# Low parts of the projection weights on VectorE in two halves, in a hybrid attention and recurrence step

## The chip, the cores and the metric

The kernel runs on one core of a Trainium2 chip. The core has five engines that run side by side, each through its own queue and in that queue's order: TensorE (PE in the profile, its weight loads PEld), VectorE (DVE), ScalarE (ACT), GpSimd (POOL) and SyncE (SP), which here issues the DMAs. The metric is the device time of one execution in microseconds (us), lower being better. The kernel before takes 2957.14 us, the median of three runs (2954.69 to 2958.95).

## The reference

One step of a diffusion backbone, one layer deep: 1024 latent tokens and 128 context tokens of width 1024 go through a feed-forward half step, a token mixer and a second feed-forward half step. All of it is float32. The mixer has two branches over the same input `h`, and each begins with a slice of one large projection:

```python
def token_mixer(h, cache, lb, w_in, ...):
    qc, kvc, kr, hq, hf_f, hf_b, hi, hgate, ga, gr = jnp.split(h @ w_in, split_idx, axis=-1)
    ...                                                  # attention: qc, kvc, kr
    q_h, v_h = jax.nn.silu(heads(hq)), heads(hi)
    f_fw = lb_h[0] + (1.0 - lb_h[0]) * jax.nn.sigmoid(heads(hf_f))
    f_bw = lb_h[1] + (1.0 - lb_h[1]) * jax.nn.sigmoid(heads(hf_b))
    o_fw, s_fw = hgrn2_chunked(q_h, 1.0 - f_fw, jnp.log(f_fw), v_h, s0[:, 0])
    o_bw, s_bw = hgrn2_chunked(flip(q_h), flip(1.0 - f_bw), flip(jnp.log(f_bw)), flip(v_h), s0[:, 1])
    o_rec = rmsnorm(o_fw + flip(o_bw), hg_norm_g) * jax.nn.silu(heads(hgate))
    merged = jax.nn.sigmoid(ga) * (o_attn @ w_up_attn) + jax.nn.sigmoid(gr) * (o_rec @ w_up_rec)
    return merged @ w_out
```

The recurrence has eight heads of 64 by 64. It carries a state S with S_t = diag(f_t) S_(t-1) + k_t v_t, where k_t = 1 - f_t, and reads it with q_t, once forwards and once backwards in time.

## The kernel before

Activations lie transposed: the 1024 features on 128 partitions in eight tiles, the 1152 tokens along the free axis, taken in three chunks of 384 (`ORDER` is 2, 0, 1).

**Split matrix products.** TensorE takes its operands as float32r, which holds fewer bits than float32. So each operand is split into a high part, which is its rounding, and a low part, which is the rest. A product becomes three (`mm3`, lines 447 to 449): high weight by high input, high weight by low input, low weight by high input. For a weight, `load_w` issues the DMA into a tile `raw` (line 241, two buffers), and `hl` makes the parts: ScalarE copies `raw` into `wh` (line 235), then GpSimd subtracts `wh` from `raw` into `wl` (line 236). `wh` and `wl` have three buffers each. A projection weight is one tile of 128 partitions by 8 by 128, so 1024 values on each partition.

**The stage of the recurrence** (`hgrn`) is where most of the changed loads are used. It computes 36 slices of the projection, each 72 matrix products: eight of the forget gates (`proj_f`), four each of queries, values and output gates (`proj_q`, `proj_v`, `proj_gate`), and sixteen of the gates that merge the branches (`proj_sg`). They are generators that yield after each half of a chunk, 12 matrix products. Between these pieces the scan of one head is woven in: `scan_pre` prepares a chunk, `scan_lev` combines blocks over four doublings, `scan_out` reads out a head. At most four slices are run per head while its three chunks are scanned.

**The scan's chain** goes over all engines. `scan_pre` forms `X` and `Y` (products of gates and their reciprocals, lines 804 to 811), the keys and queries `Kb` and `Qb` (lines 816 and 817, VectorE, two halves of the partitions each), the block factors `TK`, `TQ` and their product (lines 821 to 825), `KE` on VectorE (829) and `QP` on GpSimd (830). Each level of `scan_lev` has TensorE multiply blocks into the PSUM tile `lv` (862), then VectorE and GpSimd scale `KE` and `QP` in place (898: three parts on VectorE, one on GpSimd), VectorE multiplies the factors `T` (899), and ScalarE copies key halves `kr` (874, 875) and finished blocks `Af` (906, 907, 912). The next level's matrix products need these. The state is carried in `scan_out` (line 936). After every second head `rec_norm` normalises the output, with logarithm and exponential on ScalarE, which loads a table of functions for each.

**What sets the order.** The code is written as one program, and the framework plans each engine's queue from it, by priorities and by its own idea of how long things take; the queues in the trace therefore do not follow the program's text line by line. Loads run ahead of their use as far as free buffers allow. Instructions wrapped in `pin` keep their written order; none of the loads changed here is pinned. On the chip every queue runs in the order planned.

The first forget gate's weight is loaded with `home="pieces"`: ScalarE copies and VectorE subtracts in two halves (lines 227 and 228). All other projection loads take the last branch of `hl`.

Of the kernel before, what the change touches and what calls it, by code (L numbers as in the profile page):

```python
# [10 lines left out]
F32R = mybir.dt.float32r  # L11
# [8 lines left out]
P = 128  # L20
D = 1024
KT = D // P
# [66 lines left out]
class Trunk:  # L89
# [125 lines left out]
    def hl(self, raw, shape, eng=None, pin=lambda i: i, home=None):  # L215
        if home == "half":
            wh, wl = [[self.half(n, F32R)[:, : D // 2] for _ in range(2)] for n in ("wxh", "wxl")]
            for v in range(2):
                src = raw[:, 0, ts(v, D // 2)]
                self.nc.scalar.copy(wh[v], src)  # L220
                self.nc.gpsimd.tensor_sub(wl[v], src, wh[v])
            return wh, wl
        if home == "pieces":
            wh, wl = [self.wp.tile(shape, F32R, tag=t, bufs=3, name=t) for t in ("wh", "wl")]
            for v in range(2):
                k = slice(4 * v, 4 * v + 4)
                self.nc.scalar.copy(wh[:, k], raw[:, k])
                self.nc.vector.tensor_sub(wl[:, k], raw[:, k], wh[:, k])
            return wh, wl
        if home:  # L230
            wh, wl = [home(n)[:, :D].rearrange("p (o d) -> p o d", o=1) for n in ("wxh", "wxl")]
        else:
            wh = self.wp.tile(shape, F32R, tag="wh", bufs=3, name="wh")
            wl = self.wp.tile(shape, F32R, tag="wl", bufs=3, name="wl")
        pin(self.nc.scalar.copy(wh, raw))  # L235
        pin((eng or self.nc.gpsimd).tensor_sub(wl, raw, wh))  # L236
        return wh, wl
# [94 lines left out]
    def alloc_h(self):  # L332
        hl = [(self.tt(F32R, f"xh{k}"), self.tt(F32R, f"xl{k}")) for k in range(KT)]
        self.xh, self.xl = zip(*hl)
# [134 lines left out]
    def down(self, ws, hs, gm, c, m, tag="dn", bufs=3):  # L469
        nc = self.nc  # L470
        lo, hi = span(c)
        cs = slice(lo, hi)
        ps = self.pp.tile([P, hi - lo], F32, tag=tag, bufs=bufs, name=tag)
        self.mm3(ps, [(wh, wl, hh[:, cs], hl[:, cs]) for (wh, wl), (hh, hl) in zip(ws, hs)])
        for a, b, s in segs(c):
            nc.vector.scalar_tensor_tensor(  # L476
                self.x[m][:, a:b],
                ps[:, a - lo : b - lo],
                self.modt[:, gm, m, s : s + 1],
                self.x[m][:, a:b],  # L480
                ALU.mult,
                ALU.add,
            )
# [39 lines left out]
    def down_final(self, ws, hs, gm):  # L523
# [4 lines left out]
        for lo, hi in FINAL:  # L528
# [5 lines left out]
            def terms(m):  # L534
                w = [(rows(wh, m), rows(wl, m)) for wh, wl in ws]
                return [(wh, wl, hh[:, lo:hi], hl[:, lo:hi]) for (wh, wl), (hh, hl) in zip(w, hs)]
# [110 lines left out]
    def proj_f(self, i, h, out):  # L647
        nc = self.nc
        fs = out["f"] = self.tt(F32, "fs")
        nc.vector.memset(fs[64:P, 0:1], 1.0)  # L650
        w = self.load_w(self.a["w_in"][i], KT, P, home="pieces" if i == 0 else None)
        for c in ORDER:
            s = self.sigm((yield from self.proj_g(w, c)))
            lo, hi = c * CW, (c + 1) * CW
            for r, o in ((slice(0, 64), 0), (slice(64, P), 1)):
                nc.scalar.activation(
                    fs[r, lo + o : hi + o], s[r], AF.Identity, scale=self.lb1[r, h : h + 1], bias=self.lb[r, h : h + 1]
                )
            yield

    def proj_q(self, i, out):
        q = out["q"] = self.tt(F32, "q")
        w = self.load_w(self.a["w_in"][i], KT, P)
        for c in ORDER:
            ps = yield from self.proj_g(w, c)
            self.nc.vector.tensor_mul(q[:, c * CW : (c + 1) * CW], ps, self.sigm(ps))  # L666
            yield

    def proj_v(self, i, out):
        nc = self.nc  # L670
        V = out["V"] = self.tt(F32, "V")
        w = self.load_w(self.a["w_in"][i], KT, P)
        for c in ORDER:
            ps = yield from self.proj_g(w, c)
            t = self.fp.tile([P, CW], F32, tag="t", bufs=3, name="t")
            nc.scalar.copy(t, ps)
            pt = self.pp.tile([P, CW], F32, tag="sm", bufs=3, name="vt")
            for j in range(3):
                nc.tensor.transpose(pt[:, ts(j, P)], t[:, ts(j, P)], self.ident)
            nc.scalar.copy(V[:, c * CW : (c + 1) * CW], pt)  # L680
            yield

    def proj_gate(self, i, p, oT):
        nc = self.nc
        w = self.load_w(self.a["w_in"][i], KT, P)
        sq = self.tt(F32, "osq")[:, :T]
        nc.scalar.activation(sq, oT[:, :T], AF.Square)
        for c in ORDER:
            ps = yield from self.proj_g(w, c)
            if c == ORDER[0]:  # L690
                self.lnexp()
                for b in ORDER:
                    self.rec_norm(b, oT, sq)
            s = self.sigm(ps)
            nc.vector.tensor_mul(s, ps, s)
            cs = slice(c * CW, (c + 1) * CW)
            nc.gpsimd.tensor_mul(s, oT[:, cs], s)
            nc.sync.dma_start(self.orec[p][:, cs], s)
            yield

    def proj_sg(self, j):
        w = self.load_w(self.a["w_in"][20 + j], KT, P)
        for c in ORDER:
            s = self.sigm((yield from self.proj_g(w, c)))
            self.nc.sync.dma_start(self.sg[j // KT, j % KT][:, c * CW : (c + 1) * CW], s)
            yield
# [1127 lines left out]
```

## Time and profile before

| | |
|---|---|
| median of three runs | 2957.14 us (2954.69 to 2958.95) |
| the profiled execution | 2961.18 us, its span 2959.4 us |
| mean granted TensorE clock | 0.985 |
| TensorE busy | 2839.9 us of the span |
| VectorE, ScalarE, GpSimd busy | 1993.1, 1285.5, 1035.0 us |
| line 236 on GpSimd, `wl`, all stages | 106 operations, 238.6 us |
| the recurrence's stage | about 850 to 1460 us after the start |

A row of a group reads: line, engine, operation, the tile written, an arrow, the tiles read, shapes, count, then busy time in us and the mean of one in ns, then the idle time of the engine just before these operations and what ended it. A row of the waits reads: who waited, for whom, the sum in us, how often, the longest. A row of the timeline reads: start and length in us, engine, line, operation, tiles, count, and in brackets the idle time before it and its releaser. A row of stretches gives the busy time of each engine in that stretch, the granted clock, and the DMAs' share.

### The profile page before, as it was taken

How to read it: one execution, taken by the hardware profiler on the slowest of the kernel's cores; microseconds unless marked ns; L12 is line 12 of the kernel's file. 1: busy time of each engine (PE TensorE's matmuls, PEld its weight loads, DVE VectorE, ACT ScalarE, POOL GpSimd, SP SyncE). 2: the span in 40 equal slices, each digit the busy share in tenths (PEclk: the TensorE clock that was granted, in tenths of full speed). 3: DMA queues.
4: the chain of work that ended last, by engine and by line, in shares of the span. 5: the costliest groups of instructions: out<-in, count | busy, mean ns of one | idle time of the engine just before them, and what ended most of it. 6: DMA issues, size and time to landing. Idle time of an engine off the chain costs nothing. (4 is left out here: it accounts for less than half of the span.)

```text
span 2959.4 us, 54352 instructions
## 1 busy us (share of the span) xinstructions
PE 2839.9 (96%) x20946; PEld 2674.2 (90%) x20946; DVE 1993.1 (67%) x4212; ACT 1285.5 (43%) x2574; POOL 1035.0 (35%) x939
## 2 busy tenths in 40 slices
PE   6999999999989999999998999999999999999998
PEld 5999999999988888888897777689999999999997
DVE  7677777677667777778356777756675665546665
ACT  6432332321275666666445777721552332232112
POOL 0133332544143333333245444532442322236431
PEclk9999999999999999999998999999999999999999
DMA  6643333643111111111110001242452222135211
GB/s 239 208 144 121 122 128 116 255 158 118 57 52 66 42 52 39 54 39 54 66 40 12 18 16 32 62 167 70 144 175 89 101 88 79 68 123 200 91 45 65
DMA packets 151491, 282.44 MB, mean 95 GB/s; under 512 B 19200, under 2 KB 83776, under 8 KB 151232
## 3 DMA queue, kind: packets, MB, share of 16 engines
q1 hardware_dynamic: 151088, 278.90, 27.4%
q8 instruction: 165, 2.70, 0.4%
q14 instruction: 94, 0.77, 0.1%
q10 hardware_dynamic: 144, 0.07, 0.0%
HBM read 215.37 MB, written 63.52 MB: 94 GB/s over the span
## 5 line engine op out<-in xcount | busy, mean ns | idle before, releaser
L1583 PE MATMUL b<-xo,wo 128*128 128x288 f32 x3552 | 484.5, 296 | 0.0
L1583 PEld LDWEIGHTS b<-xo,wo 128*128 128x128 f32 x3552 | 476.4, 188 | 0.0
L476 DVE SCALAR_TENSOR_TENSOR x<-dn,modt,x 128x256 f32<-128x256 f32 (+4 forms) x728 | 353.4, 505 | 168.9 <-PE dn L449 168.0
L236 POOL TENSOR_TENSOR wl<-raw,wh 128x1024 fp32r<-128x1024 f32 (+1 forms) x106 | 238.6, 2251 | 408.7 <-ACT wh L235 405.8
L447 PE MATMUL mm<-xh,wh 128*128 128x384 f32 (+1 forms) x1008 | 365.2, 362 | 8.0 <-DVE q L666 3.9
L1583 PE MATMUL b<-bh,wo 128*128 128x288 f32 x1776 | 366.4, 295 | 1.0 <-ACT et L1593 1.0
L449 PE MATMUL mm<-xh,wl 128*128 128x384 f32 (+1 forms) x1008 | 344.8, 342 | 2.0 <-POOL wl L236 1.9
L448 PE MATMUL mm<-xl,wh 128*128 128x384 f32 (+1 forms) x1008 | 345.0, 342 | 0.0
L1583 PEld LDWEIGHTS b<-bh,wo 128*128 128x128 f32 x1776 | 289.2, 188 | 1.3 <-ACT et L1593 1.3
L1583 PE MATMUL b<-bl,wo 128*128 128x288 f32 x888 | 261.9, 295 | 0.0
L1558 ACT CAST wo<-raw 128x512 fp32r<-128x512 f32 x185 | 114.7, 621 | 230.0 <-PE b L1583 120.1
L447 PEld LDWEIGHTS mm<-xh,wh 128*128 128x128 f32 (+1 forms) x1008 | 191.5, 190 | 21.9 <-DVE q L666 4.3
L235 ACT CAST wh<-raw 128x1024 fp32r<-128x1024 f32 (+1 forms) x108 | 104.3, 968 | 244.0 <-PE dn L448 168.2
L447 PE MATMUL dn<-hh,wh 128*128 128x384 f32 (+2 forms) x576 | 196.2, 341 | 1.3 <-DVE et L1599 0.9
L1559 DVE TENSOR_TENSOR wo<-raw,wo 128x512 fp32r<-128x512 f32 x185 | 127.1, 688 | 104.4 <-ACT wo L1558 101.5
L449 PE MATMUL dn<-hh,wl 128*128 128x384 f32 (+2 forms) x576 | 194.6, 338 | 1.0 <-POOL wl L236 1.0
L449 PEld LDWEIGHTS mm<-xh,wl 128*128 128x128 f32 (+1 forms) x1008 | 191.8, 190 | 3.6 <-POOL wl L236 2.2
L448 PE MATMUL dn<-hl,wh 128*128 128x384 f32 (+2 forms) x576 | 194.3, 337 | 0.0
L448 PEld LDWEIGHTS mm<-xl,wh 128*128 128x128 f32 (+1 forms) x1008 | 192.0, 191 | 2.0 <-issue 0.4
L1661 POOL TENSOR_TENSOR hl<-hr,hh 128x1152 fp32r<-128x1152 f32 x44 | 117.9, 2690 | 196.6 <-ACT hh L1660 102.3
L1554 POOL TENSOR_TENSOR ws<-raw 128x256 f32<-128x256 f32 x74 | 70.1, 966 | 292.8 <-DMA raw<-in_w 263.2
L1315 POOL TENSOR_TENSOR ehl<-e,ehl 128x512 fp32r<-128x512 f32 x93 | 122.2, 1318 | 141.1 <-ACT ehl L1313 77.9
(389 smaller groups left out, 7069.6 us busy)
## 6 DMA issues: line engine op xcount, KB each, us to landing
raw<-in_w SPq DMA_DIRECT2D x148, 256.0 KB, 3.2
raw<-in_w SPq DMA_DIRECT2D x58, 512.0 KB, 3.4
wada<-in_w_aT SPq DMA_DIRECT2D x112, 256.0 KB, 2.9
hr<-hs SPq DMA_DIRECT2D x44, 576.0 KB, 5.0
hs<-et SPq DMA_DIRECT2D x148, 144.0 KB, 1.7
raw<-in_w_in SPq DMA_DIRECT2D x41, 512.0 KB, 3.3
hb<-hd SPq DMA_DIRECT2D x44, 288.0 KB, 3.2
x<-in_xT SPq DMA_DIRECT2D x16, 576.0 KB, 6.4
```

The costliest lines, as they stand in the source:

```text
L235: pin(self.nc.scalar.copy(wh, raw))
L236: pin((eng or self.nc.gpsimd).tensor_sub(wl, raw, wh))
L447: pin(nc.tensor.matmul(ps, wh, xh, start=start and i == 0, stop=False))
L448: pin(nc.tensor.matmul(ps, wh, xl, start=False, stop=False))
L449: pin(nc.tensor.matmul(ps, wl, xh, start=False, stop=stop and i == n - 1))
L476: nc.vector.scalar_tensor_tensor(self.x[m][:, a:b], ps[:, a - lo : b - lo], self.modt[:, gm, m, s : s + 1], self.x[m][:, a:b], ALU.mult, A ...
L1315: eng.tensor_sub(el, e, eh)
L1554: nc.gpsimd.tensor_tensor(o[:, c], x[:, c], y[:, c], op)
L1558: nc.scalar.copy(wh, src[i])
L1559: nc.vector.tensor_sub(wl, src[i], wh)
L1583: nc.tensor.matmul(ps, w[:, k], x[:, k, :QW], start=first, stop=last, skip_group_check=home != i)
L1661: nc.gpsimd.tensor_sub(hl, raw, hh)
```

## The change

`hl` gets a branch `"low"`. It takes `wh` and `wl` from the same pools as before, has ScalarE copy the whole weight, and has VectorE subtract in two halves of four tiles each, 512 values on each partition. Five generators of the recurrence's stage ask for it: `proj_f` for every head but the first, `proj_q`, `proj_v`, `proj_gate` and `proj_sg`, 35 loads in all. The attention's loads, the feed-forward's and the merge's stay with GpSimd.

```diff
             return wh, wl
+        if home == "low":
+            wh, wl = [self.wp.tile(shape, F32R, tag=t, bufs=3, name=t) for t in ("wh", "wl")]
+            self.nc.scalar.copy(wh, raw)
+            for v in range(2):
+                k = slice(4 * v, 4 * v + 4)
+                self.nc.vector.tensor_sub(wl[:, k], raw[:, k], wh[:, k])
+            return wh, wl
         if home:
...
     def proj_f(self, i, h, out):
-        w = self.load_w(self.a["w_in"][i], KT, P, home="pieces" if i == 0 else None)
+        w = self.load_w(self.a["w_in"][i], KT, P, home="pieces" if i == 0 else "low")
...
     def proj_q(self, i, out):        # and proj_v, proj_gate
-        w = self.load_w(self.a["w_in"][i], KT, P)
+        w = self.load_w(self.a["w_in"][i], KT, P, home="low")
...
     def proj_sg(self, j):
-        w = self.load_w(self.a["w_in"][20 + j], KT, P)
+        w = self.load_w(self.a["w_in"][20 + j], KT, P, home="low")
```

More of the change, by code (lines that the diff above doesn't have):

```diff
@@ L671, in proj_v @@
         V = out["V"] = self.tt(F32, "V")
-        w = self.load_w(self.a["w_in"][i], KT, P)
+        w = self.load_w(self.a["w_in"][i], KT, P, home="low")
         for c in ORDER:
@@ L684, in proj_gate @@
         nc = self.nc
-        w = self.load_w(self.a["w_in"][i], KT, P)
+        w = self.load_w(self.a["w_in"][i], KT, P, home="low")
         sq = self.tt(F32, "osq")[:, :T]
```

## The prediction

> **What bounds the kernel now.** I read five views in this order: the page's first part (who is busy), busy time by stage, the waits of TensorE in the stage that the change touches, that stage's groups kept apart by shape, and its timeline around a few of the moved instructions.
>
> ```profile
> span 2959.4 us, 54352 instructions
> PE 2839.9 (96%) x20946; PEld 2674.2 (90%) x20946; DVE 1993.1 (67%) x4212; ACT 1285.5 (43%) x2574; POOL 1035.0 (35%) x939
> ```
>
> TensorE sets the pace of the whole. So I ask of each edit only what it does to the gaps in TensorE's queue. One row of the view by stretches (columns: stretch, its length, busy time of PE, PEld, DVE, ACT and POOL, granted clock, DMA share, GB/s):
>
> ```profile
> 850.00:1460.00 610.00, 567.16 (x6203) 506.01 (x6204) 444.65 (x1014) 380.17 (x902) 204.10 (x241) 0.98 0.14 48
> ```
>
> 850 to 1460 us is the recurrence with its projections: TensorE is idle for 610.00 - 567.16 = 42.8 us there, and VectorE is busy 444.65 of 610 us (73%). What ended most of those gaps (engine and line that waited, releaser, us in total, times, longest):
>
> ```profile
> PE lv L862 <- ACT Af L906: 14.4, 9, 3.0
> PE lv L862 <- POOL QP L898: 10.3, 8, 1.3
> PE mm L447 <- DVE q L666: 3.9, 2, 2.2
> PE lv L862 <- DVE QP L898: 3.5, 7, 0.6
> ```
>
> None waits for a weight's low part. They wait for the scan's chain, which runs over VectorE, ScalarE and GpSimd. The groups of the stage (count, busy us, mean ns, idle before):
>
> ```profile
> L236 POOL TENSOR_TENSOR wl<-raw,wh 128x1024 fp32r<-128x1024 f32 x33 | 81.7, 2476 | 138.7 <-ACT wh L235 138.6
> L817 DVE TENSOR_TENSOR Qb<-qx,Y 64x384 f32<-64x384 f32 x24 | 29.3, 1223 | 0.3
> L817 DVE TENSOR_TENSOR Qb<-qx,X 64x384 f32<-64x384 f32 x24 | 13.3, 553 | 0.1
> L899 DVE TENSOR_TENSOR T<-T 128x24 f32<-128x24 f32 x24 | 19.1, 798 | 1.1
> L899 DVE TENSOR_TENSOR T<-T 128x12 f32<-128x12 f32 x24 | 4.4, 182 | 1.2
> L825 DVE TENSOR_TENSOR T<-TK,TQ 128x48 f32<-128x48 f32 x24 | 17.8, 742 | 0.5
> L823 DVE TENSOR_TENSOR TQ<-X,fs 64x48 f32<-64x48 f32 x24 | 14.6, 607 | 0.4
> ```
>
> The two L817 groups are the same operation on the same shape, and one takes 1223 ns, the other 553. A product of 24 elements takes 798 ns, one of 12 takes 182. The timeline at the start of a head says why (start, length; POOL, DVE, PE and ACT in turn):
>
> ```profile
> 1111.54 2.74 POOL L236 TENSOR_TENSOR wl<-raw,wh 128x1024 fp32r<-128x1024 f32 x1 [12.52 <-ACT wh L235]
> 1115.81 0.91 POOL L830 TENSOR_TENSOR QP<-Qb,TQ 128x384 f32<-128x384 f32 x1 [1.53 <-DVE Qb L817]
> ...
> 1111.13 0.43 DVE L869 COPY_PREDICATED A<-mask,lv 128x96 f32<-128x96 uint8 x2 [5.88 <-PE lv L862]
> 1111.47 0.55 DVE L816 TENSOR_TENSOR Kb<-kk,X 64x384 f32<-64x384 f32 x1
> 1111.94 2.75 DVE L817 TENSOR_TENSOR Qb<-qx,Y 64x384 f32<-64x384 f32 x1
> ...
> 1117.36 0.33 PE L862 MATMUL lv<-QP,kr 128*32 128x32 f32 x16 [1.33 <-POOL QP L898]
> ...
> 1110.41 1.05 ACT L235 CAST wh<-raw 128x1024 fp32r<-128x1024 f32 x1 [1.26 <-PE mm L448]
> ```
>
> While GpSimd subtracts from 1111.54 to 1114.28, a VectorE product that started meanwhile ends only at 1114.69: 2.75 us for work of 0.55. The chain goes on: Qb, then GpSimd's QP at 1115.81, then TensorE at 1117.36 after 1.33 us idle. So the subtractions are already paid for on VectorE, though they run on GpSimd.
>
> The Trainium skill, SBUF — State Buffer, section "SBUF: two separate sides", says that a GpSimd operation and a VectorE operation with two SBUF inputs take one shared port pair as "an exclusive lock, not a bandwidth split". The rows above agree: 2.75 us against 0.55.
>
> **The change part by part.** It moves 35 subtractions (7 of f, 4 each of q, v and gate, 16 of the merge gates) from GpSimd to VectorE, each cut in two 128x512 halves. The copy on ScalarE stays whole, as do the load on SP's queue and TensorE's work.
>
> For that I need the same operations undisturbed, and the subtraction as VectorE does it elsewhere:
>
> ```profile
> 1131.37 0.26 DVE L824 TENSOR_TENSOR TQ<-Y,fs 64x48 f32<-64x48 f32 x1
> 1131.66 0.21 DVE L825 TENSOR_TENSOR T<-TK,TQ 128x48 f32<-128x48 f32 x1
> 1131.91 0.59 DVE L899 TENSOR_TENSOR T<-T 128x24 f32<-128x24 f32 x3
> ...
> L1559 DVE TENSOR_TENSOR wo<-raw,wo 128x512 fp32r<-128x512 f32 x185 | 127.1, 688 | 104.4 <-ACT wo L1558 101.5
> L1559 DVE TENSOR_TENSOR wo<-ws,wo 128x512 fp32r<-128x512 f32 x74 | 70.5, 952 | 100.4 <-ACT wo L1558 100.3
> ```
>
> *Taken from GpSimd:* 35 x 2.476 = 86.7 us. GpSimd is 33% busy in the stage, so this alone is worth nothing. What counts is the hold on VectorE that ends. A lower bound from four groups, mean less undisturbed value, times 24: L817 (1.223 - 0.553), 16.1 us; L899 (0.798 - 0.182), 14.8; L825, 742 less about 210 ns (at 1131.66), 12.8; L823, 607 less about 260 (its twin L824 at 1131.37), 8.3. Together 52 us. An upper bound is the whole 81.7.
>
> *Added to VectorE:* L1559 is the same subtraction in the feed-forward stage, same shape and types: 688 ns, or 952 where GpSimd works on the same tiles. So 70 halves cost 48.2 us, at most 66.6. I take 688, since GpSimd then has only short operations left. Per weight: 1.38 us of VectorE in place of about 2.2 lost (2.75 - 0.55), so its chain moves 0.8 us forward. Between the bounds VectorE wins up to 81.7 - 48.2 = 33 us and loses up to 66.6 - 52 = 15.
>
> Now where this lies on TensorE's path:
>
> (a) *Heads that start as at 1111.* The eight waits for POOL QP, 10.3 us, are four of 1.33 of this shape (the last is shown here) and four others of 1.25 on average.
>
> ```profile
> 1417.12 0.38 PE L862 MATMUL lv<-QP,kr 128*32 128x32 f32 x21 [1.33 <-POOL QP L898]
> ```
>
> Each shrinks by 0.8 of its 1.33 us if both halves run ahead of Qb, and vanishes if they run behind it. I take 4 x 0.8 = 3.2 us.
>
> (b) *The end of a block, three times, as at 1077:*
>
> ```profile
> 1076.40 0.86 DVE L825 TENSOR_TENSOR T<-TK,TQ 128x48 f32<-128x48 f32 x1
> 1077.30 2.70 DVE L899 TENSOR_TENSOR T<-T 128x24 f32<-128x24 f32 x3
> ...
> 1085.81 0.40 PE L862 MATMUL lv<-QP,kr 128*32 128x32 f32 x24 [0.57 <-DVE QP L898]
> 1089.13 0.39 PE L862 MATMUL lv<-QP,kr 64*32 64x32 f32 x22 [0.45 <-DVE QP L898]
> 1093.53 0.56 PE L862 MATMUL lv<-QP,kr 64*64 64x64 f32 x10 [1.46 <-ACT Af L906]
> ```
>
> L825 and L899 take 3.56 us here and 0.80 at 1131; with the halves, 2.18. VectorE gains 1.38, which covers the waits of 0.57 and 0.45 (three such pairs make 3.1 of the 3.5 us of waits for DVE QP). The 1.46 ends on ScalarE, and I count nothing of it: 3 x 1.0 = 3.1 us.
>
> (c) *The norm of the recurrence, three times.* TensorE waits longest here, on ScalarE:
>
> ```profile
> 1040.30:1048.60 8.30, 6.59 (x61) 5.66 (x59) 5.49 (x12) 8.16 (x13) 2.12 (x3) 1.00 0.01 2
> 1048.60:1055.40 6.80, 5.56 (x22) 5.35 (x23) 5.02 (x10) 5.40 (x15) 1.93 (x3) 0.50 0.08 29
> ...
> 1049.84 0.58 PE L862 MATMUL lv<-QP,kr 64*64 64x64 f32 x3 [2.95 <-ACT Af L906]
> ```
>
> ScalarE is full (8.16 of 8.30) ahead of the wait, and its queue began late, behind a Qb of kind (a). Some of the 0.8 us may reach here: 0 to 0.8, I take 0.4, three times 1.2 us. After each wait the clock is 0.50 for 6.8 us, worth some 3.4; I leave that as it is.
>
> The Trainium skill, TensorE: Matmul & The Clock Gate, section "What's actually happening", gives a free-running window of about 3.4 us in which an idle TensorE falls to half rate. By it a wait cut to 2.5 us fills no window and spares the slow stretch, so that the sum would be 9.0 + 3 x 3.4 = 19 us. The rows bear this out only in part: the clock is halved here after 2.95 us of idling, less than the page's window.
>
> (d) *The first q weight:* needed the moment it is ready.
>
> ```profile
> 839.75 2.36 POOL L236 TENSOR_TENSOR wl<-raw,wh 128x1024 fp32r<-128x1024 f32 x1 [0.77 <-ACT wh L235]
> 842.16 0.69 PE L449 MATMUL mm<-xh,wl 128*128 128x384 f32 x1 [1.86 <-POOL wl L236]
> 845.09 0.17 DVE L612 MEMSET onesb<- 128x128 f32 x1 [5.53 <-POOL xl L398]
> ```
>
> VectorE is free for the 5.53 us up to 845.09, so the first half, begun like GpSimd's at 839.75, is done near 840.4 instead of 842.1. TensorE's 1.86 us shrink to about 0.1: 1.8 us.
>
> (e) *Costs.* One subtraction near 888.6 delays nothing today (VectorE runs reciprocals through it), and its 1.38 us will cost; the one before it, at 885, gives back as much: 0. VectorE now holds GpSimd in turn: 33 x 1.38 = 45.5 us of 610, 7.5% of the time, and a GpSimd operation that meets a half waits 0.35 us on average; on the 95 QP operations that is 2.5 us, of which the share on the path is small: 0.3 us lost. If VectorE loses this cover, it costs all 2.5. New waits: each half is queued on VectorE behind ScalarE's copy, and what stands behind it there is the scan's chain; I price that as a rival. SP's next load waits for the raw tile:
>
> ```profile
> SPq L241 <- POOL wl L236: 204.2, 32, 18.4
> ```
>
> It is released 1 us earlier (1.38 against 2.4). No large wait of TensorE in the stage is for a weight, so nothing hangs on it.
>
> Sum: 3.2 + 3.1 + 1.2 + 1.8 - 0.3 = 9.0 us. The profiled execution took 2961.18 us (its span of 2959.4 and 1.8 around it), so it would take 2952.2. The median of the three runs is 4.0 us below that execution, which gives 2948.
>
> **The rivals.** *More than that:* the planner puts the halves into VectorE's idle times rather than ahead of the chain. For it: VectorE is idle 165 us in the stage. Then (a) yields 4 x 1.33, (b) also its 1.46 us three times, and one or two slow-clock stretches go: 9.0 + 2.1 + 4.4 + 5 = 20 us, 2937.
>
> *No change:* the chain comes forward, but another releaser ends last. For it: 14.4 us of TensorE's waits, the largest row, end on ScalarE already, and ScalarE is full ahead of the longest. Only (d) is left, some 2 us: 2955.
>
> *Slower: VectorE stands at the head of its queue, waiting for the copy.* VectorE runs in order, so a half that is queued early holds the scan behind it until ScalarE has made the high part. For it: GpSimd today waits 138.6 us for that copy at its 33 subtractions, and the copy itself waits for TensorE to free a buffer (1.26 us at 1110). Against it: at 1111 VectorE is idle until 1111.13 and the copy ends at 1111.46, so 0.3 us would be lost there. It decides once a wait exceeds 2.2 - 1.38 = 0.8 us on average. With a full copy (1.05) and its 1.26 each weight costs 1.38 + 2.31 - 2.2 = 1.5 us, in the stretches where VectorE has no slack, some 8 of 33, 12 us, and one more slow-clock stretch of 3.4: 2957 + 15 = 2972.
>
> *The lock turned round* is a mechanism of its own: halves hold GpSimd's QP in front of TensorE. If each of the eight POOL QP waits grew by a half of 0.69 us, 5.5 us would be lost of the 9: 2954, within no change. The Trainium skill's SBUF page, same section, is behind it: whoever starts first keeps the ports for the whole instruction.
>
> **How the numbers follow.** Forecast 0.43 (2943 to 2953 by itself), more 0.15, no change and the lock turned round together 0.14, slower 0.28. What a measurement here can tell from no change is 0.2%, 5.9 us. The forecast case falls short of it at times, so faster is 0.56, same 0.16, slower 0.28. The range reaches from some way past the better rival, 2934, to the slower one, 2972.
>
> **What would show it.** No VectorE product of the scan takes over 2 us any more; mean of L817 Qb from 1223 to under 650 ns, of L825 and L899 to under 300; new 128x512 subtractions near 0.69 us; VectorE's busy time in the stage lower by 7 us or more; TensorE's waits for POOL QP and DVE QP down from 13.8 to under 8 us. I am wrong if VectorE shows waits for ScalarE's copy of several us in sum, if TensorE waits for low parts, or if the order of the queues in the stage has changed so much that waits stand in new places.

## The result, and the profile after

The changed kernel takes 2933.47 us (median of four runs, 2932.25 to 2934.04) against 2957.40 us (2954.69 to 2958.95): a ratio of 0.992, interval 0.9902 to 0.9937, 23.9 us less. Run again beside other runs of the kernel before, it took 2930.96 against 2957.94: 0.9906, interval 0.9889 to 0.9923. The forecast was 2948 us, in a range of 2934 to 2972: the direction was right, the size far too small, and the time lies half a microsecond below the range. In the changed kernel, line numbers from `hl` on are higher by 7: what was L817 is L824, L862 is L869, L899 is L906. The subtractions on VectorE are L235, the copy on ScalarE L232.

The profiled execution took 2932.25 us. Its page's first part:

```profile
span 2930.1 us, 54396 instructions
PE 2833.2 (97%) x20946; PEld 2668.0 (91%) x20946; DVE 1976.7 (67%) x4282; ACT 1285.9 (44%) x2574; POOL 957.3 (33%) x904
```

VectorE has 70 more instructions (4212 to 4282) and yet is busy 16 us less. Where the time went is seen by stretches (stretch, length, busy time of PE, PEld, DVE, ACT, POOL, clock, DMA share, GB/s). First the kernel before, from the start of the stage's first loads to its end:

```profile
750.00:1460.00 710.00, 662.13 (x6716) 598.24 (x6716) 511.49 (x1164) 423.94 (x982) 235.24 (x263) 0.98 0.15 52
```

Nearly the same work, by the count of TensorE's instructions (6716 and 6712), in the kernel after; then its part from 850 us on, as in the prediction:

```profile
750.00:1434.00 684.00, 654.05 (x6712) 590.64 (x6711) 494.58 (x1230) 424.66 (x982) 157.48 (x228) 0.99 0.16 54
850.00:1434.00 584.00, 557.32 (x6185) 496.64 (x6184) 425.40 (x1078) 377.24 (x897) 130.61 (x208) 0.99 0.15 50
```

710 us became 684. Paired instruction by instruction (see below), 24.6 of the 29 us between the two profiled executions lie in this stage. Another 1.7 us arose before 750 us and 3.1 behind 1460 us, where no changed load is used. They are not put down to the change: two profiled executions of the changed kernel differ by 1.9 us at 750 us alone. Over the paired instructions of the stage TensorE's idle time fell from 47.9 to 30.0 us, by 17.9. The other 6.7 us are the same instructions running in less time, which fits the clock: in this stage the half-rate stretches were 34 us long in all before (seven places, of 3.4 or 6.8 us each), with TensorE busy for 30.8 us of them, and 17 us after (five of 3.4), with TensorE busy for 16.7. Half of the 14.1 us saved is 7.

The waits of TensorE in the stage, after (engine and line that waited, releaser, us in total, times, longest):

```profile
PE lv L869 <- ACT Af L913: 10.3, 9, 1.6
PE mm L454 <- DVE q L673: 3.7, 2, 2.5
...
PE lv L869 <- DVE QP L905: 1.8, 5, 0.7
...
PE lv L869 <- POOL QP L905: 1.1, 1, 1.1
```

The waits for QP, 13.8 us before, are 2.9; those for Af fell from 14.4 to 10.3, none longer than 1.6. The groups by shape say why:

```profile
L235 DVE TENSOR_TENSOR wl<-raw,wh 128x512 fp32r<-128x512 f32 x66 | 44.4, 692 | 5.1 <-ACT wh L232 4.6
L824 DVE TENSOR_TENSOR Qb<-qx,Y 64x384 f32<-64x384 f32 x24 | 15.3, 639 | 0.3
L906 DVE TENSOR_TENSOR T<-T 128x24 f32<-128x24 f32 x24 | 4.9, 204 | 1.3 <-DVE T L832 0.5
L832 DVE TENSOR_TENSOR T<-TK,TQ 128x48 f32<-128x48 f32 x24 | 8.9, 371 | 0.5
L830 DVE TENSOR_TENSOR TQ<-X,fs 64x48 f32<-64x48 f32 x24 | 6.0, 248 | 0.4
```

Most of the scan's products now run near the speed of their undisturbed twins: Qb 639 ns instead of 1223, T 204 instead of 798. The product of line 832 stays at 371 ns, where its twin took 210; what still holds it shows in the last experiment. And VectorE hardly waits for the high part: 4.6 us at 66 halves, where GpSimd waited 138.6.

**Which waits went.** TensorE's instructions of both traces were paired one by one; the order is the same but for a few swaps in the first head (860 to 893 us). So the difference of the start times can be followed, and it grows in steps. The last column says by how much the wait shrank:

| place (time before) | what ended there | us |
|---|---|---|
| 842.16 | first q weight (d) | 1.8 |
| 968.03, 1117.36, 1267.15, 1417.12 | start of a head, POOL QP (a) | 4 x 1.33 = 5.3 |
| 990.65, 1140.01, 1289.77 | the other waits for POOL QP | 3.3 in all |
| 1049.84, 1199.23, 1348.96 | the norm, ACT Af (c) | 3 x 1.37 = 4.1 |
| near 1086 to 1089, 1236, 1384 | end of a block, DVE QP (b) | 2.7 in all |

That is 17.2 us of the 17.9 by which TensorE's idle time fell. The first head (843 to 967 us) is not in the table: single waits there come and go, by up to 3.1 us, and in sum 0.8 us ends. One of the new waits is the 1.1 us for POOL QP. Shortly ahead of it a half of the subtraction and GpSimd's QP run side by side, and that QP takes 1.36 us, where it took 0.89 before:

```profile
894.85 0.69 DVE L235 TENSOR_TENSOR wl<-raw,wh 128x512 fp32r<-128x512 f32 x1
...
894.90 1.36 POOL L837 TENSOR_TENSOR QP<-Qb,TQ 128x384 f32<-128x384 f32 x1 [3.00 <-DVE TQ L831]
```

The start of a head, after, that answers to 1111 us of before (VectorE, GpSimd and TensorE in turn):

```profile
1099.49 0.54 DVE L824 TENSOR_TENSOR Qb<-qx,Y 64x384 f32<-64x384 f32 x1
1100.05 0.56 DVE L823 TENSOR_TENSOR Kb<-kk,Y 64x384 f32<-64x384 f32 x1
1100.53 0.55 DVE L824 TENSOR_TENSOR Qb<-qx,X 64x384 f32<-64x384 f32 x1
1101.11 0.69 DVE L235 TENSOR_TENSOR wl<-raw,wh 128x512 fp32r<-128x512 f32 x1
...
1103.74 0.69 DVE L235 TENSOR_TENSOR wl<-raw,wh 128x512 fp32r<-128x512 f32 x1
...
1101.16 1.37 POOL L837 TENSOR_TENSOR QP<-Qb,TQ 128x384 f32<-128x384 f32 x1 [16.95 <-DVE Qb L824]
...
1103.51 0.40 PE L869 MATMUL lv<-QP,kr 128*32 128x32 f32 x24
```

The first Qb takes 0.54 us instead of 2.75. Both halves of the subtraction stand *behind* the two Qb, so the whole 2.2 us reach GpSimd's QP (in all seven places where this Qb took over 2 us before, they now start 1.6 and 4.2 us after it), and TensorE's 1.33 us of waiting are gone, though QP itself is now held by the first half: 1.37 us, where it took 0.91.

### The profile page after: what moved, and what is told of

Read it like the earlier page. It is cut to its first block, busy times and chain, and to the rows that moved or that the text cites. A ratio compares the mean times of both kernels' runs of the same rounds, so it can differ in the third digit from the quotient of the medians.

```text
span 2930.1 us, 54396 instructions
## 1 busy us (share of the span) xinstructions
PE 2833.2 (97%) x20946; PEld 2668.0 (91%) x20946; DVE 1976.7 (67%) x4282; ACT 1285.9 (44%) x2574; POOL 957.3 (33%) x904
## 5 line engine op out<-in xcount | busy, mean ns | idle before, releaser
L243 POOL TENSOR_TENSOR wl<-raw,wh 128x1024 fp32r<-128x1024 f32 (+3 forms) x71 | 152.0, 2142 | 267.8 <-ACT wh L242 265.0
L314 DVE SCALAR_TENSOR_TENSOR junk<-wada,cb 128x512 bf16<-128x512 f32 x224 | 165.0, 737 | 7.1 <-DMA wada<-in_w_aT 6.3
L1590 PEld LDWEIGHTS b<-bl,wo 128*128 128x128 f32 x888 | 167.4, 189 | 0.0
```

The lines of the kernel that those rows point to most:

```text
L314: nc.vector.scalar_tensor_tensor(junk, ws[n % 2], 1.0, cs[s], ALU.mult, ALU.mult, accum_out=o)
L1590: nc.tensor.matmul(ps, w[:, k], x[:, k, :QW], start=first, stop=last, skip_group_check=home != i)
```

## The experiments

All edits are to the changed kernel. The theory, called A in the expectations, is that GpSimd's subtraction holds VectorE's two-input operations, and that the end of this hold is the gain. The rivals: that the planned order of the queues changed (B), that GpSimd or its queue was simply too busy, and that the cutting in two helped.

### The hold put back, with nothing else changed

GpSimd makes the same subtraction beside VectorE's halves, into a tile that nobody reads.

```diff
         self.nc.vector.tensor_sub(wl[:, k], raw[:, k], wh[:, k])
+    junk = self.fp.tile(shape, F32R, tag="junk", bufs=1, name="junk")
+    self.nc.gpsimd.tensor_sub(junk, raw, wh)
     return wh, wl
```

> The changed kernel with a second, useless subtraction of the whole weight on GpSimd beside the two halves on VectorE (35 more GpSimd operations of 128x1024, result thrown away). The order planned for TensorE, ScalarE and VectorE is that of the changed kernel, instruction for instruction. Theory A (the gain is the end of the hold that GpSimd's subtraction has on VectorE's two-input operations): the hold is back and VectorE's own halves stay, so all of the 24 us is lost and more: 2957 to 2972 us, and scan products on VectorE of over 2 us are back. Theory B (the gain comes from the new order of the queues): nothing is lost, 2933 us. Theory C (GpSimd's queue alone, its QP operations standing behind subtractions): the part that ended on POOL QP comes back, 4 x 1.4 + 3 x 1.1 = 9 us: 2942 us.

Measured: 2980.46 us against 2958.27, ratio 1.0077 (1.0062 to 1.0092). The order of TensorE's, ScalarE's and VectorE's instructions is that of the changed kernel. All of the gain is gone, and 22 us more, which is beyond the range expected of A. The groups of the stage and TensorE's waits:

```profile
L237 POOL TENSOR_TENSOR junk<-raw,wh 128x1024 fp32r<-128x1024 f32 x33 | 83.6, 2532 | 138.8 <-issue 100.6 <-ACT wh L232 38.1
L235 DVE TENSOR_TENSOR wl<-raw,wh 128x512 fp32r<-128x512 f32 x66 | 59.2, 916 | 6.4 <-ACT wh L232 5.9
L826 DVE TENSOR_TENSOR Qb<-qx,Y 64x384 f32<-64x384 f32 x24 | 29.7, 1239 | 0.3
```

```profile
PE lv L871 <- POOL QP L907: 15.0, 12, 1.8
PE lv L871 <- ACT Af L915: 13.3, 9, 3.0
PE lv L871 <- DVE QP L907: 11.3, 11, 1.9
```

Qb is back at 1239 ns, the waits for QP are back and nearly double those of before (26.3 us in place of 13.8), the waits for Af are again up to 3.0 us. VectorE's own halves are held too: 916 ns instead of 692. That it is worse than the kernel before fits VectorE having both the hold and the 44 us of new work; no run takes the two apart. B would have left the time near 2933: it falls. The Trainium skill, SBUF — State Buffer, section "SBUF: two separate sides", calls such a hold an exclusive lock between a GpSimd operation that reads SBUF and a VectorE operation with two SBUF inputs; the 1239 against 639 ns agree.

### No subtraction at all

```diff
-    for v in range(2):
-        k = slice(4 * v, 4 * v + 4)
-        self.nc.vector.tensor_sub(wl[:, k], raw[:, k], wh[:, k])
-    return wh, wl
+    return wh, wh
```

> No subtraction at all for the 35 weights: the high part is used in place of the low part (the correction by the weights' low parts is left out of these products). It prices the 48 us of work that VectorE took over. Theory A: the hold is gone as in the changed kernel, and the halves lie on the chain in few places: 2922 to 2930 us, 4 to 11 us below the changed kernel. If VectorE's work were hidden altogether: 2933 us. If it were fully on the path (33 x 1.38 = 45 us): under 2895 us.

Measured: 2924.39 us against 2958.27, ratio 0.9886 (0.987 to 0.9903). This is the ceiling: taken away altogether, the subtractions are worth 33.9 us. VectorE's work of 48 us gives 9.1 of these back (2933.47 - 2924.39), less than a fifth of its length; the changed kernel's second median, 2930.96, would make it 6.6. The stage's row also gives a second measure of the hold:

```profile
850.00:1425.00 575.00, 556.07 (x6194) 496.38 (x6195) 383.44 (x1013) 379.78 (x901) 123.60 (x208) 0.99 0.15 51
```

VectorE is busy 383.44 us in the stage without any subtraction, and was 444.65 before with the same work: the hold was 61 us. From the changed kernel it comes out at 64.9 (444.65 less 425.40, plus 66 halves of 0.692, 45.7).

### The cutting in two, without the move, and the move without the cutting

```diff
-        self.nc.vector.tensor_sub(wl[:, k], raw[:, k], wh[:, k])
+        self.nc.gpsimd.tensor_sub(wl[:, k], raw[:, k], wh[:, k])
```

> The changed kernel with its two halves on GpSimd again. Theory A: the holds are there, each shorter (about 1.25 us) and twice as many, so little is gained: 2948 to 2958 us. Rival (the cut in two is what helps): 2933 to 2940 us.

Measured: 2958.42 us against 2958.27, ratio 1.0002 (0.9992 to 1.0011): no gain. Each hold is shorter, but there are twice as many:

```profile
L235 POOL TENSOR_TENSOR wl<-raw,wh 128x512 fp32r<-128x512 f32 x66 | 89.6, 1376 | 135.8 <-ACT wh L232 135.6
L824 DVE TENSOR_TENSOR Qb<-qx,Y 64x384 f32<-64x384 f32 x24 | 22.0, 918 | 1.2 <-ACT qx L807 0.9
```

The single Qb is held less (918 ns instead of 1223), but VectorE's busy time in the stage hardly falls, 441.30 us where it was 444.65:

```profile
850.00:1460.00 610.00, 567.88 (x6221) 506.17 (x6220) 441.30 (x1016) 382.02 (x905) 214.16 (x276) 0.98 0.15 49
```

```diff
-    for v in range(2):
-        k = slice(4 * v, 4 * v + 4)
-        self.nc.vector.tensor_sub(wl[:, k], raw[:, k], wh[:, k])
+    self.nc.vector.tensor_sub(wl, raw, wh)
```

> The changed kernel with the subtraction on VectorE in one piece of 128x1024 (about 1.22 us) in place of two halves. Theory A: no difference that matters, 2930 to 2937 us. Rival (the cut in two is what helps): the scan stands behind longer pieces and a good part of the gain goes, 2942 to 2955 us.

Measured: 2934.57 us against 2958.27, ratio 0.9921 (0.9906 to 0.9936): all of the gain. So the engine matters, and the size of the pieces doesn't.

### GpSimd busy, but reading nothing

```diff
+    junk = self.fp.tile(shape, F32, tag="junk", bufs=1, name="junk")
+    for v in range(2):
+        self.nc.gpsimd.memset(junk, 0.0)
     return wh, wl
```

> The changed kernel with two useless fills of a 128x1024 tile on GpSimd at each of the 35 weights. GpSimd is busy again for some 1.8 us per weight, but reads nothing from SBUF. If the hold comes from GpSimd being busy or from its queue (what stands behind it there waits): 2942 us or more, and long products on VectorE. If it comes from GpSimd reading operands (Theory A as narrowed by the skill's rule): VectorE's products stay under 1 us, only QP behind the fills is late: 2933 to 2942 us.

Measured: 2945.17 us against 2956.97, ratio 0.9961 (0.9946 to 0.9975), which neither theory had quite right. The fills keep GpSimd busy for 62 us, and VectorE's products are not held:

```profile
L238 POOL MEMSET junk<- 128x1024 f32 x65 | 61.9, 952 | 2.0
...
L827 DVE TENSOR_TENSOR Qb<-qx,Y 64x384 f32<-64x384 f32 x24 | 14.9, 622 | 0.3
L909 DVE TENSOR_TENSOR T<-T 128x24 f32<-128x24 f32 x24 | 5.3, 223 | 1.3 <-DVE T L835 0.5
```

The time lost against the changed kernel lies in the first head. Two stretches of this kernel, and the same two of the changed one:

```profile
750.00:930.00 180.00, 159.63 (x1093) 151.72 (x1092) 130.47 (x288) 96.37 (x198) 108.00 (x120) 0.96 0.17 57
930.00:1460.00 530.00, 512.07 (x5750) 455.05 (x5750) 375.26 (x958) 333.23 (x797) 113.19 (x181) 0.99 0.16 53
```

```profile
750.00:930.00 180.00, 168.13 (x1234) 159.12 (x1234) 134.00 (x311) 102.66 (x214) 52.06 (x56) 0.98 0.18 63
930.00:1460.00 530.00, 511.91 (x5651) 455.50 (x5650) 364.50 (x933) 337.14 (x793) 110.78 (x176) 0.99 0.15 52
```

Until 930 us TensorE gets 8.5 us less done; after that it is as busy as in the changed kernel (512.07 and 511.91). So in the other heads a busy GpSimd costs nothing, and the hold of line 236 is one of reading. This too agrees with the Trainium skill, SBUF — State Buffer, section "SBUF: two separate sides", which limits the lock against a VectorE operation with two SBUF inputs to GpSimd operations that read SBUF.

The loss in the first head is one of GpSimd's queue. The fills wait for no copy, so eleven of them run in one go, and GpSimd's next low part of the input, `xl`, stands behind them until 855.12. VectorE waits for that, its queries `q` come late, and TensorE waits for them (GpSimd, VectorE and TensorE in turn):

```profile
844.09 11.06 POOL L238 MEMSET junk<- 128x1024 f32 x11
...
856.14 1.33 DVE L396 TENSOR_TENSOR xn<-x,rs 128x384 f32<-128x384 f32 x1 [3.94 <-POOL xl L408]
...
858.00 0.69 PE L457 MATMUL mm<-xh,wh 128*128 128x384 f32 x1 [6.79 <-DVE q L676]
```

### What VectorE's time costs

The halves are made twice, the second time into a spare tile.

```diff
         self.nc.vector.tensor_sub(wl[:, k], raw[:, k], wh[:, k])
+    junk = self.fp.tile(shape, F32R, tag="junk", bufs=1, name="junk")
+    for v in range(2):
+        k = slice(4 * v, 4 * v + 4)
+        self.nc.vector.tensor_sub(junk[:, k], raw[:, k], wh[:, k])
```

> The changed kernel with VectorE's halves done twice (the second result is thrown away): 48 us more on VectorE. Without any subtraction the time was 2924.4 us, with one 2933.5: 9.1 us for the first 48 us. If VectorE still has slack, the second 48 us cost about as much, 2940 to 2946 us; if the slack is used up, up to the whole 48: 2960 us and over.

Measured: 2941.32 us against 2956.97, ratio 0.9949 (0.9934 to 0.9964): 7.9 us above the changed kernel's first result, 10.4 above its second, for 48 us of work. The first 48 us cost 9.1 or 6.6. The two together cost 16.9 us for 96, so VectorE's slack takes about four fifths of the work. What does come through shows in the waits of TensorE for VectorE's QP, 5.6 us in place of 1.8:

```profile
PE lv L873 <- DVE QP L909: 5.6, 11, 1.7
```

### Which of the weights

The sixteen merge gates go back to GpSimd.

```diff
     def proj_sg(self, j):
-        w = self.load_w(self.a["w_in"][20 + j], KT, P, home="low")
+        w = self.load_w(self.a["w_in"][20 + j], KT, P)
```

> The sixteen merge-gate weights back on GpSimd, the other nineteen on VectorE. If every weight is worth the same: 24 x 16/35 = 11 us are lost, 2944 us. If the gain sits in a few places of each pair of heads and those are not the merge gates': 2933 to 2938 us; if they are: 2950 us and over.

Measured: 2949.49 us against 2957.94, ratio 0.9974 (0.9965 to 0.9983). The changed kernel beside it took 2930.96. So 18.5 of its 27 us are lost with 16 of 35 weights; by their number it would be 12.3. The time stands between the case of equal shares (2944) and the one in which the merge gates carry the gain (2950 and over), close to the second. With 16 of the stage's 33 subtractions on GpSimd again (the first row counts two more, of the merge), Qb is held somewhat more than half as much as before, 978 ns on average between 639 and 1223:

```profile
L243 POOL TENSOR_TENSOR wl<-raw,wh 128x1024 fp32r<-128x1024 f32 x18 | 44.3, 2461 | 103.5 <-ACT wh L242 103.5
L824 DVE TENSOR_TENSOR Qb<-qx,Y 64x384 f32<-64x384 f32 x24 | 23.5, 978 | 0.3
```

```profile
PE lv L869 <- ACT Af L913: 14.9, 10, 3.0
PE lv L869 <- POOL QP L905: 7.2, 5, 2.1
```

The 3.0 us waits at the norm are back, and with them the 14.9 us for Af.

### More of GpSimd's products to VectorE, and the changed kernel again

The first edit moves the products that form `Y`, the second the first product of QP:

```diff
-        for out, pos, off, eng in ((X, (2, 1, 0), 1, nc.vector), (Y, (4, 5, 6, 7), 0, nc.gpsimd)):
+        for out, pos, off, eng in ((X, (2, 1, 0), 1, nc.vector), (Y, (4, 5, 6, 7), 0, nc.vector)):
```

> The changed kernel with the three products of Y per chunk (line 815, 72 of 0.39 us on GpSimd) on VectorE too. Theory A taken further: 28 us of GpSimd reading ends, VectorE gets 72 x about 0.26 = 19 us: 2930 to 2936 us. If VectorE is by now the tighter engine: 2936 to 2945 us.

```diff
-        nc.gpsimd.tensor_tensor(e8(qp), e8(Qb), bc(TQ, 8), ALU.mult)
+        nc.vector.tensor_tensor(e8(qp), e8(Qb), bc(TQ, 8), ALU.mult)
```

> The changed kernel with the first product of QP per chunk (line 837, 24 of 1.12 us on GpSimd) on VectorE, 24 x 0.56 = 13 us there. It stands between Qb and TensorE's wait for POOL QP. Theory A taken further: 2929 to 2934 us. If VectorE is the tighter engine: 2935 to 2942 us.

Measured: 2934.11 us (ratio 0.9922, 0.9908 to 0.9937) and 2930.05 us (0.9909, 0.9894 to 0.9924), both against 2956.97. The second seemed 3 us ahead, so it was run again with the changed kernel beside it.

> The changed kernel as it is, beside the next run, for a closer comparison: 2933 us by its own median of four runs.

> The changed kernel with the first product of QP per chunk on VectorE, a second time and beside the changed kernel. If its lead of 3.4 us (2930.05 against 2933.47, measured apart) is real: 2 to 5 us below the run beside it. If it was the difference between two sessions: within 1.5 us.

Measured: 2930.96 and 2929.77 us against 2957.94, ratios 0.9906 (0.9889 to 0.9923) and 0.9907 (0.9892 to 0.9921). They are 1.2 us apart, so no lead is shown. With QP on VectorE the product of line 832 falls further:

```profile
L837 DVE TENSOR_TENSOR QP<-Qb,TQ 128x384 f32<-128x384 f32 x24 | 13.4, 560 | 0.3
L832 DVE TENSOR_TENSOR T<-TK,TQ 128x48 f32<-128x48 f32 x24 | 4.9, 205 | 0.4
```

4.0 us of hold on T end (371 to 205 ns, 24 times), for 13.4 us of new work. No version that computes the same is shown to beat the changed kernel.

## Why the prediction was right and wrong

**The mechanism: right, and shown.** The prediction said that the subtractions "are already paid for on VectorE, though they run on GpSimd". The hold put back loses everything; the move alone, uncut, gives everything. The bounds held: hold 61 to 65 us (52 to 81.7 forecast), halves 692 ns (688), VectorE's busy time in the stage 19 us lower (at least 7). Of the signs that it named, one did not come: the product of L825 was to fall under 300 ns and stayed at 371, since GpSimd's QP still holds it.

**What failed is the size on TensorE's path.** Two steps had it wrong: the choice that the halves run ahead of Qb, so that 0.8 us of the 2.2 reach the next engine, and the decision to count nothing for four of the QP waits and for the clock. Term by term:

**(a), "0.8 if both halves run ahead of Qb": mis-sized, 3.2 for 5.3 us.** The choice fell on the wrong end of its own two. The halves run behind Qb, and each of the four waits ended.

**(a) again, the "four others of 1.25 on average": left at nothing, 3.3 us.** One of the four lies in the first head; the other three make the 3.3 us. Nothing visible stands directly ahead of them; the hold lay 8 to 11 us earlier on the chain. They are the wait at 990.65 and its like in the next pairs of heads, at 1140.01 and 1289.77. The wait at 990.65 before, and the product that led up to the one at 1140.01:

```profile
990.65 0.39 PE L862 MATMUL lv<-QP,kr 64*32 64x32 f32 x24 [1.21 <-POOL QP L898]
...
1128.97 2.39 DVE L823 TENSOR_TENSOR TQ<-X,fs 64x48 f32<-64x48 f32 x1
```

After, the same product:

```profile
1115.31 0.25 DVE L830 TENSOR_TENSOR TQ<-X,fs 64x48 f32<-64x48 f32 x1
```

**(b): right in mechanism and nearly in size**, 2.7 for 3.1 us; the wait for Af behind it stayed, as predicted (nine waits, up to 1.6).

**(c), "0 to 0.8, I take 0.4, three times 1.2 us": mis-sized, 4.1 us.** The prediction took only a share of the 0.8 us for the way over ScalarE. But all of the 2.2 us of the held Qb reached ScalarE's queue. Its first copy at the norm, before:

```profile
1037.53 0.51 ACT L800 COPY qx<-q 64x384 f32<-64x384 f32 x1 [3.78 <-DVE Qb L817]
```

After, with a new wait of ScalarE, the wait of TensorE that followed, and then the stretch behind it (the clock is the third figure from the end):

```profile
1026.11 0.51 ACT L807 COPY qx<-q 64x384 f32<-64x384 f32 x1 [1.58 <-DVE Qb L824]
...
1028.63 0.49 ACT L651 ACTIVATE sg<-mm 128x384 f32<-128x384 f32 x1 [0.84 <-PE mm L456]
...
1039.25 0.56 PE L869 MATMUL lv<-QP,kr 64*64 64x64 f32 x6 [1.58 <-ACT Af L913]
```

```profile
1040.50:1043.90 3.40, 3.40 (x14) 3.30 (x13) 2.18 (x4) 2.46 (x5) 1.25 (x1) 0.50 0.00 0
```

ScalarE's wait fell from 3.78 to 1.58 us, by 2.2, but TensorE's from 2.95 to 1.58, by 1.37. The difference is the 0.84 us that ScalarE now waits for TensorE at 1028.63: it had come so far forward that its next input was not ready. From there on ScalarE is full, and what was left, 1.37 us, came out whole at the end. The other two norms show the same.

**(c), the clock, "I leave that as it is": left at nothing, 6.7 us.** This is the largest term that was missing. The prediction put a slow stretch of 6.8 us behind each norm; they were 6.8, 6.8 and 3.4 us, and after the change 3.4 each. The other 10 us of slow time that went lie elsewhere, near 840, 892 and 1393 us. The Trainium skill, TensorE: Matmul & The Clock Gate, section "What's actually happening", had spoken for a gain here, as the prediction said, and by it the sum would have been 19 us. Its direction was right. The reading that the prediction made of it, that a wait cut to less than a window of about 3.4 us spares the slow stretch, is not what the trace shows: the clock is halved after 1.58 us of waiting too. Only the lengths of the slow stretches, 3.4 and twice 3.4 us, agree with the window. Nor does such a wait always bring one: in the second profiled execution of the changed kernel (run again beside the last experiment) TensorE waits 1.57 us at the same place, until 1041.18, and the clock stays at 1.00:

```profile
1041.20:1045.00 3.80, 3.80 (x26) 3.63 (x26) 2.15 (x6) 3.65 (x8) 0.42 (x1) 1.00 0.09 32
```

So a single pair of executions says little about the clock. Over all executions with a recorded clock its mean was 0.9866 before (34 executions), 0.9896 after (8) and 0.985 with the hold put back (4). The 0.0030 between the first two are some 9 us of 2930, an estimate for the whole kernel. No run here moved the clock by itself, so that this term follows from the shorter waits is argued, not shown.

**(d): right**, 1.8 us for 1.8.

**(e): right that it is small**, but its size was off. The halves do hold GpSimd: its 24 first QP products went from 958 to 1118 ns and its 95 others from 584 to 619, together 7 us for the 2.5 forecast. On TensorE's path this shows in the new wait of 1.1 us for GpSimd's QP in the first head, where 0.3 us was forecast in all.

**The rivals.** *More than that*, 20 us, was nearest, and mostly for the reason that it gave: halves behind the chain, full waits at the heads, slow stretches gone. That its sum came so close is in part luck, since its 4.4 us for Af at the ends of the blocks did not come, while 3.3 us at other waits and 4.1 at the norms did. *Slower* asked for waits of over 0.8 us per weight at the head of VectorE's queue; they were 4.6 us in all. *The lock turned round* exists, as at 1101.16, where it costs TensorE nothing, and at 894.90, where a wait of TensorE follows. Taken together: terms forecast at 9.3 us gave 13.9; the waits not counted gave 3.3, the first head 0.8 and the clock 6.7, some 24.6 us in the stage of the profiled executions. The whole difference of these executions, 29 us, is 5 more than that of the medians, since the profiled run before was 4 us above its median and that after 1 us below.

## What to carry to other kernels

Compare the mean of an operation with that of its twin on the same shape: where it is twice as long, look at what another engine does meanwhile, for the price of that engine's work may lie on the one that is held. Then follow a removed delay through every queue on the way, at its full size, up to the point where another wait takes its place: here 2.2 us left VectorE, ScalarE lost 0.84 of them to a wait for TensorE, and 1.37 arrived. An engine's added work can cost far less than its length while it has slack: here 48 us of VectorE cost 7 to 10.

## What the chip showed beside this

In these traces GpSimd's operations hold VectorE's two-input products only where they read: 65 fills of 128x1024, 952 ns each, left Qb at 622 ns, where subtractions of the same tile's size put it at 1239. Cutting such a subtraction in two makes GpSimd slower in sum (66 operations of 1376 ns on average, 89.6 us in place of 81.7) and frees only 3 us of VectorE. And moving 45 us of work onto VectorE made it less busy, 425.40 us in the stage where it was 444.65.
